# Sums of SBUF operands to VectorE, a changed product order and later memory values in a one-core decoder block

## The chip, the cores and the metric

The kernel runs on one core of a Trainium2 chip as one launch. The metric is device time in microseconds (us): 2584.59 us is the median of three runs (2582.75 to 2585.81). Engines are named as in the profile: PE (TensorE matmuls), PEld (its weight loads), DVE (VectorE), ACT (ScalarE), POOL (GpSimd), SP (the queue that issues DMAs).

## The reference, cut to what matters

One decoder block over 1024 tokens of width 1024, everything in fp32:

```python
x = x + 0.5 * swiglu(rmsnorm(x, ffn1_norm), ffn1_w_gate, ffn1_w_up, ffn1_w_down)      # FFN1, width 2816
x = x + hybrid_mixer(rmsnorm(x, mix_norm), ...)     # two attentions, gates, output projection
x = x + memory_cross_attention(rmsnorm(x, mem_q_norm), rmsnorm(mem, mem_kv_norm), ...)  # 256 memory tokens
x = x + 0.5 * swiglu(rmsnorm(x, ffn2_norm), ffn2_w_gate, ffn2_w_up, ffn2_w_down)      # FFN2
return rmsnorm(x, final_norm)
# swiglu: (silu(h @ w_gate) * (h @ w_up)) @ w_down;  memory: k, v = split(mem_n @ w_kv)
```

## The kernel before, in words

Every matrix product is made of three matmuls: each operand is split into a rounded part (an ACT copy, "hi") and the rest (a DVE subtraction, "lo"), and `mm3` (L375 to L377) multiplies hi by hi, hi by lo and lo by hi. Such a subtraction is called a split below.

The FFN projections use a scheme with seven products in place of eight (Strassen's, in Winograd's manner). Its left operand is the weights, its right operand the normalised tokens, each cut into 2 x 2 blocks. A block sum is needed for most products: of weights (`left_sums`, tile ws, then split into wf), of tokens (`norm_forms`, tile fs, then split into F, the "forms"), and in the down projection of weights again (tile da) and of gated results (tile gs). `sum_on` (L485 to L493) makes such a sum and lets the planner choose POOL or DVE. The token halves are tiles 0 to 3 and 4 to 7. Products 3 and 5 need forms of the second half alone (tiles R), product 4 and 2 the first half (tiles xs), products 1, 6 and 7 both.

`ffn_up` runs 11 steps; each step makes a gate projection (called g below) and an up projection (u) of one pair of column groups by `seven`, so 14 products of 12 matmuls of 512 columns: g3 g5 g4 g2 g1 g6 g7, then u3 to u7 in the same manner. After a product DVE or ACT takes its bank on (vt L535, L541, L545; sg L596, L599). `ffn_down` has seven stages of 11 such units for four banks. Before FFN1, `memory_kv` normalises the 256 memory tokens (xn, mT), makes eight key units (each 24 matmuls of 256 columns, results cc to DRAM) and two value groups (each 48 matmuls of 512 columns). Before FFN2, `out_proj` adds the cross attention to x tile by tile (x L1327), and each finished tile is normalised (ACT square, POOL rstd L439 and L440, DVE xn L444), transposed on PE (T), copied and turned into forms.

The order on each engine is no loop order. Every operation goes to a planner (`Plan`) with an assumed cost per engine and a rank, its due time, which advances with the assumed matmul times. `Plan.order` takes the operation with the lowest rank among those that could start next on the engine that comes free first, within 60 ns, and looks for free buffers in pools (`TAGS`, `POOLS`). Each engine then runs its list strictly in order, and so does the DMA queue SP. The lines that set it here are these:

```python
self.plan.op({"POOL": 2.9 * n + 50, "DVE": 1.04 * n + 157}, f, reads, writes, self.r if rank is None else rank)  # sum_on
for f in self.memory_kv(40.0): f()                 # keys and values, before the tokens
```

Of the kernel before, what the change touches and what calls it, by code (L numbers as in the profile page):

```python
# [10 lines left out]
F32 = mybir.dt.float32  # L11
# [8 lines left out]
P = 128  # L20
# [141 lines left out]
class Plan:  # L162
# [152 lines left out]
class Block:  # L315
# [46 lines left out]
    def dve(self, ns, run, reads, writes, rank=None):  # L362
        self.plan.op({"DVE": ns}, lambda _: run(), reads, writes, self.r if rank is None else rank)
# [39 lines left out]
    def weight(self, key, lead=14.0, pool=False):  # L403
# [20 lines left out]
    def rms(self, x, g, out, parts=1):  # L424

        nc, n = self.nc, D // parts
        st = self.buf("sm")
        cut = lambda b, j: b()[:, j * n:(j + 1) * n]
        key = lambda j: j if parts > 1 else None
        for j in range(parts):  # L430
            def square(j=j):

                nc.scalar.activation(cut(out, j), cut(x, j), AF.Square, scale=1.0 / math.sqrt(D), accum_out=st()[:, j:j + 1])
            self.act(n, square, [(x, key(j))], [(out, key(j)), (st, j)], sbuf=True, acc=True)

        def rstd():
            if parts > 1:
                nc.gpsimd.tensor_tensor(st()[:, 0:1], st()[:, 0:1], st()[:, 1:2], op=ALU.add)
            nc.gpsimd.tensor_scalar_add(st()[:, 2:3], st()[:, 0:1], EPS)  # L439
            nc.gpsimd.tensor_tensor(st()[:, 3:4], st()[:, 2:3], self.mhalf, op=ALU.pow)  # L440
        self.pool(425 + 220 * parts, rstd, [], [st])
        for j in range(parts):
            def scale(j=j):
                nc.vector.scalar_tensor_tensor(cut(out, j), cut(x, j), st()[:, 3:4], cut(g, j), op0=ALU.mult, op1=ALU.mult)  # L444
            self.dve(1.042 * n + 130, scale, [x, st, g], [(out, key(j))])

    def norm_T(self, x, g, put, writes, key):

        xn = self.buf("xn")
        self.rms(x, g, xn)  # L450
# [35 lines left out]
    def sum_on(self, n, out, a, b, sign, reads, writes, rank=None):  # L486

        nc = self.nc
        op = ALU.add if sign > 0 else ALU.subtract

        def f(en):
            (nc.vector if en == "DVE" else nc.gpsimd).tensor_tensor(out(), a(), b(), op=op)  # L492
        self.plan.op({"POOL": 2.9 * n + 50, "DVE": 1.04 * n + 157}, f, reads, writes, self.r if rank is None else rank)  # L493

    def left_sums(self, key0, key1, lead=12.0):
# [4 lines left out]
        for b, key in zip(raw, (key0, key1)):  # L500
            self.dma(524288, lambda b=b, key=key: nc.sync.dma_start(b(), self.io["w"][self.index[key]]), [], [b], self.r - lead - 8)
        quarter = lambda ij: raw[ij[0]]()[:, ij[1] * 512:ij[1] * 512 + 512]

        def make(i):
# [9 lines left out]
            self.dve(690, lambda: nc.vector.tensor_sub(w()[:, 512:1024], val(), w()[:, 0:512].bitcast(F32)),  # L514
# [4 lines left out]
    def seven(self, key0, key1, F, use):  # L519
# [3 lines left out]
        make = self.left_sums(key0, key1)  # L523
# [21 lines left out]
        self.dve(690, lambda: nc.vector.tensor_add(v(), x(), v()), [x], [(vt, 0)])  # L545
        product(6, y, False)
        self.dve(690, lambda: sub(d, y), [y, (vt, 0)], [(vt, 1)])
        use(1, 1, d, [(vt, 1)])
        product(7, z, False)
        self.dve(690, lambda: sub(v, z), [z], [(vt, 0)])  # L550
        use(0, 0, v, [(vt, 0)])

    def norm_forms(self, x, g, F, t):
# [3 lines left out]
        self.rms(x, g, xn)  # L557
# [13 lines left out]
        for i in (5, 3) if half else (4, 2, 1, 6, 7):  # L571
            parts = F.SUMS[i]
            src = [(F.raw[4 * ij[1] + t % 4], ij[0]) for ij in parts[:2]]
            if len(parts) == 1:
                val, rd = lambda parts=parts: part(parts[0]), src
            else:
                s = self.buf("fs")
                self.sum_on(512, s, lambda parts=parts: part(parts[0]), lambda parts=parts: part(parts[1]), parts[2], src, [s])
                val, rd = s, [s]
# [3 lines left out]
                       [(b, t % 4) for b in F.t[i][1]], count=2, sbuf=True)  # L583


    def ffn_up(self, n, F):
# [4 lines left out]
        for c in range(H):  # L591
# [6 lines left out]
            def up(i, j, view, reads, sg=sg, at=at):  # L598
                self.dve(690, lambda: nc.vector.tensor_mul(at(i, j), at(i, j), view()), reads, [(sg[i], j)])  # L599
            self.seven(("g" + n, c), ("g" + n, c + H), F, gate)  # L600
            self.seven(("u" + n, c), ("u" + n, c + H), F, up)
            for i, parts in self.LEFT.items():
# [9 lines left out]
                self.dma(262144, lambda i=i, c=c, val=val: nc.sync.dma_start(gd[i]()[c], val()), rd, [(gd[i], c)])  # L612
        return gd

    def ffn_down(self, n, gd, x, done):
# [10 lines left out]
        def load(i, k, m, lead=10.0):  # L626
# [18 lines left out]
            for b, tag in ((raw, "gf"), (src[0], "df")):  # L645
# [3 lines left out]
                self.dve(1.04 * w + 157, lambda b=b, hl=hl: nc.vector.tensor_sub(  # L649
# [26 lines left out]
        def into(t, bank, tb, ch, s):  # L676
            def f():
                xs = x[tb]()[:, ch * 512:ch * 512 + 512]
                stt(xs, bank[t](), xs, s)
            self.dve(690, f, [bank[t]], [(x[tb], ch)])  # L680
# [6 lines left out]
        stage(3, z, True, lambda t: self.dve(690, lambda: stt(v(t), z[t](), v(t), 0.5), [z[t]], [vk(t)]))  # L687
        stage(4, y2, True, lambda t: self.dve(690, lambda: stt(v(t), y2[t](), v(t), 0.5), [y2[t]], [vk(t)]))
# [11 lines left out]
    def memory_kv(self, lead):  # L700
# [4 lines left out]
        g = self.gain("mem_kv_norm")  # L705
        for t in range(2):
# [16 lines left out]
        def values(ch):  # L723
            pv = [self.buf("mm") for _ in range(2)]
# [693 lines left out]
    def run(self):  # L1418
# [23 lines left out]
        for f in self.memory_kv(40.0):  # L1442
            f()
        r = self.r
        self.r = 2.0
        g = self.gain("ffn1_norm", 0.0)
        x = load(lambda t: io["x"][t], order=late, lead=2.0, step=2.0)
# [8 lines left out]
        gd = self.ffn_up("1", F)  # L1456
# [27 lines left out]
        self.out_proj("mo", o, x, done, late=True)  # L1484
# [20 lines left out]
G0 = 3  # L1505
# [22 lines left out]
```

## Time and profile before

| | us |
|---|---|
| median of three runs | 2584.59 |
| the profiled execution | 2588.4 |
| its span, first to last instruction | 2586.4 |
| PE busy | 2522.5 (98%) |
| DVE busy | 1664.6 (64%) |
| ACT busy | 1180.9 (46%) |
| POOL busy | 619.3 (24%) |

All times in rows are from the span's start. A timeline row gives start, duration, engine, line, operation, out<-in, count, and in brackets the idle time before it with what ended it. Durations of instructions that follow each other overlap by up to 0.08 us, so the time that one takes on its engine is the distance to the next start. PEclk is the granted clock of TensorE: 1.00 is the upper of its two levels, 2.4 GHz, and 0.5 the lower, 1.2 GHz.

### The profile page before, as it was taken

The page shows a single profiled execution, that of the slowest core. Times are in us where ns is not written, and L with a number is a line of the kernel's source. Part 1 is how long each engine was busy: PE and PEld are TensorE (multiplying, and loading weights), DVE is VectorE, ACT ScalarE, POOL GpSimd, SP SyncE. Part 2 cuts the span into 40 slices and gives each one's busy share as a digit, 9 for nine tenths or more (in the row PEclk, how much of TensorE's full clock was granted, in tenths as well). Part 3 has the DMA queues.
Part 4 walks back from the last instruction along what each step waited for, and adds up shares of the span by engine and source line. Part 5 has one row for each costly group of instructions (what it writes and reads, how often), then busy time and mean ns, then how long its engine had stood idle before and what let it go on. Part 6 is the DMA issues. An engine that isn't in the chain of part 4 may idle for free.

```text
span 2586.4 us, 34955 instructions
## 1 busy us (share of the span) xinstructions
PE 2522.5 (98%) x12613; PEld 2132.7 (82%) x12613; DVE 1664.6 (64%) x3120; ACT 1180.9 (46%) x2352; POOL 619.3 (24%) x590
## 2 busy tenths in 40 slices
PE   7899999999999999999999999999998999999998
PEld 6688888888788888898888888888876888888887
DVE  8755556667765477788766766344576556557566
ACT  6422232334445567777776753233443232233433
POOL 5643344331200001111000003000034334332313
PEclk9999999999999999999999999999998999999999
DMA  7233233696722110210212344241112223327964
GB/s 280 98 114 114 78 131 118 205 369 225 266 82 83 45 58 30 72 63 19 79 53 82 116 137 155 82 147 57 50 74 86 97 103 106 123 93 271 343 234 164
DMA packets 137485, 329.90 MB, mean 128 GB/s; under 512 B 14656, under 2 KB 18096, under 8 KB 137184
## 3 DMA queue, kind: packets, MB, share of 16 engines
q1 hardware_dynamic: 137248, 327.47, 36.5%
q8 instruction: 99, 1.62, 0.3%
q14 instruction: 74, 0.61, 0.1%
q0 software_dynamic: 64, 0.20, 0.0%
HBM read 254.17 MB, written 75.02 MB: 127 GB/s over the span
## 4 chain that ended last, share of the span: by engine, by line
PE 89%; DVE 3%; ACT 2%; DMA 1%; issue 1%; POOL 0%; SPq 0%; DVEq 0%; POOLq 0%; ACTq 0%
PE z L375 11%; PE z L376 11%; PE z L377 11%; PE mm L375 7%; PE mm L376 7%; PE mm L377 7%; PE y L376 5%; PE y L375 5%; PE y L377 5%; PE T L381 4%; PE pv L1124 4%; PE acc L377 2%; PE acc L375 2%; PE acc L376 2%; PE s L1049 2%; PE s L1050 2%
## 5 line engine op out<-in xcount | busy, mean ns | idle before, releaser
L375 PE MATMUL z<-F,wf 128*128 128x512 f32 x1232 | 483.1, 392 | 15.0 <-ACT wf L513 5.0
L377 PE MATMUL z<-F,wf 128*128 128x512 f32 x1232 | 482.0, 391 | 3.5 <-DVE wf L514 3.5
L376 PE MATMUL z<-F,wf 128*128 128x512 f32 x1232 | 482.6, 392 | 2.5 <-DVE F L397 2.4
L492 POOL TENSOR_TENSOR ws<-wa 128x512 f32<-128x512 f32 x197 | 285.7, 1465 | 507.6 <-DVE wf L514 333.6
L375 PEld LDWEIGHTS z<-F,wf 128*128 128x128 f32 x1232 | 232.8, 189 | 66.7 <-ACT wf L513 5.5
L375 PE MATMUL mm<-h,w 128*128 128x512 f32 x704 | 286.8, 407 | 0.0
L377 PE MATMUL mm<-h,w 128*128 128x512 f32 x704 | 276.5, 393 | 0.0
L376 PE MATMUL mm<-h,w 128*128 128x512 f32 x704 | 276.4, 393 | 0.0
L377 PEld LDWEIGHTS z<-F,wf 128*128 128x128 f32 x1232 | 232.7, 189 | 52.7 <-DVE wf L514 4.6
L376 PEld LDWEIGHTS z<-F,wf 128*128 128x128 f32 x1232 | 232.8, 189 | 52.2 <-DVE F L397 4.0
L376 PE MATMUL y<-df,gf 128*128 128x512 f32 x616 | 239.9, 389 | 1.1 <-DVE df L649 1.1
L375 PE MATMUL y<-df,gf 128*128 128x512 f32 x616 | 240.4, 390 | 0.0
L377 PE MATMUL y<-df,gf 128*128 128x512 f32 x616 | 239.9, 389 | 0.0
L514 DVE TENSOR_TENSOR wf<-ws,wf 128x512 fp32r<-128x512 f32 x220 | 170.7, 777 | 48.8 <-ACT wf L513 48.8
L397 DVE TENSOR_TENSOR pt<-T,pt 128x512 fp32r<-128x512 f32 (+1 forms) x264 | 156.2, 614 | 68.4 <-ACT pt L390 67.3
L390 ACT CAST pt<-T 128x512 fp32r<-128x512 f32 (+1 forms) x264 | 132.3, 528 | 77.5 <-PE T L381 75.5
L1077 ACT ACTIVATE p<-p,sm 128x128 f32<-128x128 f32 (+7 forms) x192 | 143.4, 747 | 46.3 <-DVE sm L1147 43.8
L377 PEld LDWEIGHTS mm<-h,w 128*128 128x128 f32 x704 | 132.6, 188 | 29.7
L513 ACT CAST wf<-ws 128x512 fp32r<-128x512 f32 x220 | 131.8, 619 | 47.4 <-PE z L377 45.5
L376 PEld LDWEIGHTS mm<-h,w 128*128 128x128 f32 x704 | 133.6, 190 | 18.8
L375 PEld LDWEIGHTS mm<-h,w 128*128 128x128 f32 x704 | 133.3, 189 | 19.0
L413 DVE TENSOR_TENSOR w<-wr,w 128x1024 fp32r<-128x1024 f32 x95 | 121.4, 1289 | 40.4 <-ACT w L409 38.7
(254 smaller groups left out, 5042.3 us busy)
## 6 DMA issues: line engine op xcount, KB each, us to landing
da<-in_w_dram SPq DMA_DIRECT2D x264, 256.0 KB, 5.9
wr<-in_w_dram SPq DMA_DIRECT2D x95, 512.0 KB, 4.7
wa<-in_w_dram SPq DMA_DIRECT2D x88, 512.0 KB, 3.9
dg<-gd SPq DMA_DIRECT2D x70, 512.0 KB, 6.0
gd<-gs SPq DMA_DIRECT2D x110, 256.0 KB, 2.1
xd<-x SPq DMA_DIRECT2D x24, 512.0 KB, 2.6
x<-xd SPq DMA_DIRECT2D x24, 512.0 KB, 5.9
gd<-sg SPq DMA_DIRECT2D x44, 256.0 KB, 2.1
```

What stands on the lines that cost most here:

```text
L375: mm(out, a[0], b[0], start=first, stop=False, skip_group_check=more)
L376: mm(out, a[0], b[1], start=False, stop=False, skip_group_check=more)
L377: mm(out, a[1], b[0], start=False, stop=last, skip_group_check=more)
L381: self.nc.tensor.transpose(out, src, self.ident[0:k, 0:k])
L390: nc.scalar.copy(h, s)
L397: nc.vector.tensor_sub(l, s, h.bitcast(F32))
L413: self.dve(1135, lambda: nc.vector.tensor_sub(lo(), raw(), hi().bitcast(F32)), [raw, hi], [lo], rank=r + 4)
L492: (nc.vector if en == "DVE" else nc.gpsimd).tensor_tensor(out(), a(), b(), op=op)
L513: self.act(512, lambda: nc.scalar.copy(w()[:, 0:512], val()), rd, [(w, 0)], sbuf=True, rank=rank + 3)
L514: self.dve(690, lambda: nc.vector.tensor_sub(w()[:, 512:1024], val(), w()[:, 0:512].bitcast(F32)), rd + [(w, 0)], [(w, 1)], rank=rank + 3)
L1077: nc.scalar.activation(p[e]()[:, 0:row[e]], p[e]()[:, 0:row[e]], AF.Exp, bias=m[e]()[:, j:j + 1], scale=-1.0, accum_out=l()[:, e:e + 1])
L1124: mm(pv()[:, 0:256], v, y()[:, b * 256:b * 256 + 256], start=unit["fresh"], stop=stop and y is lo)
```

## The change

It has four parts. All sums of two SBUF operands go to DVE, with the assumed costs of DVE operations made smaller. In `ffn_up` the first step makes g3, g5, u3 and u5 before the rest (`apart`, `AHEAD`), and reads the first weight unit a second time for that. The forms of the first half have later due times (`LATER`), and `rms` tells the planner that the normalised tile is 1 us later (`slack`, in `norm_T` and `norm_forms`). The memory's normalised tokens are written to DRAM (md); the keys are made first, and each value group reads the tokens back and runs inside FFN1, ahead of steps 2 and 3.

```diff
-    "F": ("u", 28), "R": ("u", 4), "wa": ("u", 4), "wf": ("u", 6), "sg": ("u", 4), "vt": ("u", 2),
-    "da": ("u", 6), "dg": ("u", 3), "df": ("u", 6), "gf": ("u", 6), "vb": ("u", 2), "xs": ("u", 3),
+    "F": ("u", 28), "R": ("u", 4), "wa": ("u", 4), "wf": ("u", 6), "sg": ("u", 4), "vt": ("u", 4),
+    "da": ("u", 6), "dg": ("u", 3), "df": ("u", 6), "gf": ("u", 6), "vb": ("u", 2), "xs": ("u", 4),
...
     def norm_T(self, x, g, put, writes, key):
-        self.rms(x, g, xn)
+        self.rms(x, g, xn, slack=1000.0)
...
-        def f(en):
-            (nc.vector if en == "DVE" else nc.gpsimd).tensor_tensor(out(), a(), b(), op=op)
-        self.plan.op({"POOL": 2.9 * n + 50, "DVE": 1.04 * n + 157}, f, reads, writes, self.r if rank is None else rank)
+        self.dve(1.04 * n + 70, lambda: nc.vector.tensor_tensor(out(), a(), b(), op=op), reads, writes, rank)
...
-    def seven(self, key0, key1, F, use):
-        make = self.left_sums(key0, key1)
+    def seven(self, key0, key1, F, use, apart=False):
+        make = self.left_sums(key0, None if apart else key1)
...
         product(5, z, False)
         use(0, 1, z, [z])
+        yield
+        if apart:
+            make = self.left_sums(key0, key1)
         product(4, y, True)
-        self.dve(690, lambda: nc.vector.tensor_add(v(), y(), v()), [y], [(vt, 0)])
+        self.dve(603, lambda: nc.vector.tensor_add(v(), y(), v()), [y], [(vt, 0)])
...
     def norm_forms(self, x, g, F, t):
-            parts = F.SUMS[i]
+            parts, rank = F.SUMS[i], self.r + LATER.get(i, 0.0)
...
     def ffn_up(self, n, F, between={}):
+        rows = [parts(c) for c in range(H)]
+        early = {c: [next(rows[c]) for _ in range(2)] for c in range(AHEAD)}
+        for c in range(AHEAD):
+            for s in early[c]:
+                next(s)
+        for c in range(H):
+            between.get(c, lambda: None)()
+            for j in range(2):
+                s = early[c][j] if c < AHEAD else next(rows[c])
+                for _ in s:
+                    pass
+            next(rows[c])
...
     def memory_kv(self, lead):
+        for s, j in ((s, j) for j in range(2) for s in range(2)):
+            self.dma(524288, lambda s=s, j=j: nc.sync.dma_start(md[s][j](), mT[s][j]().bitcast(F32)), [mT[s][j]], [md[s][j]])
...
         def values(ch):
+            mT = [[self.buf("mT", F32R) for _ in range(2)] for _ in range(2)]
+            for s, j in ((s, j) for j in range(2) for s in range(2)):
+                self.dma(524288, lambda s=s, j=j: nc.sync.dma_start(mT[s][j]().bitcast(F32), md[s][j]()), [md[s][j]], [mT[s][j]],
+                         self.r - 12)
...
-        for f in self.memory_kv(40.0):
+        keys = self.memory_kv(0.0)
+        values = [keys.pop(), keys.pop()][::-1]
+        for f in keys:
             f()
...
-        gd = self.ffn_up("1", F)
+        gd = self.ffn_up("1", F, {2: values[0], 3: values[1]})
...
+G0, AHEAD = 3, 1
+LATER = {4: 8.0, 2: 11.0, 1: 14.0, 6: 17.0, 7: 20.0}
```

How this moves instructions is seen best on DVE. The first place is the start of FFN1, where the last form splits stand. Before, the queue has the splits of forms (F), mixed with weight splits (wf); the first results of a product (vt) come only after the last F:

```order
L397 TENSOR_TENSOR F<-fs,F 128x2x128 x8
L514 TENSOR_TENSOR wf<-wa,wf 128x512
L397 TENSOR_TENSOR cc<-mm,cc 128x512
L397 TENSOR_TENSOR F<-xs,F 128x2x128 x2
L397 TENSOR_TENSOR F<-fs,F 128x2x128 x2
L514 TENSOR_TENSOR wf<-ws,wf 128x512
L492 TENSOR_TENSOR fs<-xs,R 128x512
L397 TENSOR_TENSOR F<-fs,F 128x2x128 x2
L514 TENSOR_TENSOR wf<-wa,wf 128x512
L397 TENSOR_TENSOR F<-fs,F 128x2x128 x4
```

Now, in the same place, sums of weights (ws) and of tokens (fs) stand in the queue too, and the results of u5 (sg) and g4 (vt) stand ahead of the last forms:

```order
L488 TENSOR_TENSOR ws<-wa 128x512
L397 TENSOR_TENSOR F<-fs,F 128x2x128 x2
L511 TENSOR_TENSOR wf<-ws,wf 128x512
L488 TENSOR_TENSOR fs<-xs,R 128x512 x3
L397 TENSOR_TENSOR F<-xs,F 128x2x128 x2
L602 TENSOR_TENSOR sg<-sg,z 128x512
L397 TENSOR_TENSOR F<-fs,F 128x2x128 x2
L511 TENSOR_TENSOR wf<-ws,wf 128x512
L488 TENSOR_TENSOR fs<-xs,R 128x512
L542 TENSOR_TENSOR vt<-z,vt 128x512
```

So products run on PE between the forms instead of behind them. The second place is the start of FFN2, where the last token tile is added (x<-acc,x), normalised (xn) and copied (xs). Before, 24 form splits and three sums stand between xn of the tile before and that add:

```order
L444 SCALAR_TENSOR_TENSOR xn<-x,sm,gain 128x1024
L397 TENSOR_TENSOR F<-fs,F 128x2x128 x8
L492 TENSOR_TENSOR fs<-xs,R 128x512
L397 TENSOR_TENSOR F<-fs,F 128x2x128 x2
L397 TENSOR_TENSOR F<-xs,F 128x2x128 x2
L397 TENSOR_TENSOR F<-fs,F 128x2x128 x4
L492 TENSOR_TENSOR fs<-xs 128x512
L492 TENSOR_TENSOR fs<-xs,R 128x512
L397 TENSOR_TENSOR F<-fs,F 128x2x128 x8
L1327 TENSOR_TENSOR x<-acc,x 128x512
L514 TENSOR_TENSOR wf<-ws,wf 128x512
```

Now three split pairs, a sum and a copy stand between them:

```order
L441 SCALAR_TENSOR_TENSOR xn<-x,sm,gain 128x1024
L397 TENSOR_TENSOR F<-fs,F 128x2x128 x2
L488 TENSOR_TENSOR fs<-xs 128x512
L397 TENSOR_TENSOR F<-fs,F 128x2x128 x2
L569 COPY xs<-T_18593 128x512
L397 TENSOR_TENSOR F<-fs,F 128x2x128 x2
L1353 TENSOR_TENSOR x<-acc,x 128x512
L397 TENSOR_TENSOR F<-fs,F 128x2x128 x2
L488 TENSOR_TENSOR fs<-xs,R 128x512
L488 TENSOR_TENSOR fs<-xs 128x512
L511 TENSOR_TENSOR wf<-ws,wf 128x512
L441 SCALAR_TENSOR_TENSOR xn<-x,sm,gain 128x1024
```

The add of the last tile has moved ahead of most forms of the tiles before it.

## Rows read from the trace of the kernel before

**Rows 1.** The page's first part: busy time, share and instructions by engine.
```profile
PE 2522.5 (98%) x12613; PEld 2132.7 (82%) x12613; DVE 1664.6 (64%) x3120; ACT 1180.9 (46%) x2352; POOL 619.3 (24%) x590
```
**Rows 2.** Busy time by stretch: length, PE, PEld, DVE, ACT, POOL, PEclk, DMA, GB/s.
```profile
0.00:65.00 65.00, 46.58 (x313) 43.58 (x313) 52.43 (x73) 44.60 (x90) 32.97 (x34) 0.99 0.76 278
65.00:130.00 65.00, 52.62 (x215) 41.33 (x214) 50.04 (x68) 30.43 (x66) 39.31 (x24) 0.93 0.29 98
...
195.00:260.00 65.00, 65.00 (x288) 53.84 (x287) 37.96 (x54) 15.71 (x30) 24.97 (x17) 1.00 0.33 114
...
520.00:585.00 65.00, 65.00 (x289) 53.83 (x288) 42.46 (x36) 27.10 (x31) 18.99 (x8) 1.00 1.01 373
```
**Rows 3.** Waits of PE over the span: us in total, times, longest.
```profile
PE T L381 <- DVE xn L444: 26.0, 7, 8.1
```
**Rows 4.** Timeline of DVE from the start into FFN1.
```profile
6.77 1.28 DVE L444 SCALAR_TENSOR_TENSOR xn<-m,sm,gain 128x1024 f32<-128x1024 f32 x1 [5.61 <-POOL sm L440]
...
11.56 1.22 DVE L413 TENSOR_TENSOR w<-wr,w 128x1024 fp32r<-128x1024 f32 x1
...
49.11 0.75 DVE L397 TENSOR_TENSOR F<-R,F 128x256 fp32r<-128x256 f32 x2
49.78 2.94 DVE L397 TENSOR_TENSOR F<-fs,F 128x256 fp32r<-128x256 f32 x2
...
54.45 1.28 DVE L492 TENSOR_TENSOR fs<-xs,R 128x512 f32<-128x512 f32 x2
...
82.49 6.02 DVE L397 TENSOR_TENSOR F<-fs,F 128x256 fp32r<-128x256 f32 x8
...
95.83 2.47 DVE L397 TENSOR_TENSOR F<-fs,F 128x256 fp32r<-128x256 f32 x2 [1.62 <-ACT F L390]
...
133.25 0.68 DVE L535 TENSOR_TENSOR vt<-vt,z 128x512 f32<-128x512 f32 x1
```
**Rows 5.** Timeline of POOL beside the eight splits at 82.49.
```profile
82.11 1.60 POOL L492 TENSOR_TENSOR fs<-xs,R 128x512 f32<-128x512 f32 x1 [1.43 <-DVE F L397]
...
86.85 1.38 POOL L492 TENSOR_TENSOR fs<-xs,R 128x512 f32<-128x512 f32 x1 [1.03 <-DVE F L397]
```
**Rows 6.** Timeline of PE in the keys.
```profile
40.03 0.28 PE L377 MATMUL mm<-mT,w 128*128 128x256 f32 x1
40.15 0.28 PE L375 MATMUL mm<-mT,w 128*128 128x256 f32 x1
```
**Rows 7.** Timeline of DVE at the start of FFN2.
```profile
1921.10 0.68 DVE L1327 TENSOR_TENSOR x<-acc,x 128x512 f32<-128x512 f32 x1
...
1941.22 0.68 DVE L1327 TENSOR_TENSOR x<-acc,x 128x512 f32<-128x512 f32 x1
...
1944.59 1.28 DVE L444 SCALAR_TENSOR_TENSOR xn<-x,sm,gain 128x1024 f32<-128x1024 f32 x1
...
1954.11 4.92 DVE L397 TENSOR_TENSOR F<-fs,F 128x256 fp32r<-128x256 f32 x8
...
1988.90 0.68 DVE L535 TENSOR_TENSOR vt<-vt,z 128x512 f32<-128x512 f32 x1
```
**Rows 8.** Busy time by stretch at the start of FFN2.
```profile
1930.00:1940.00 10.00, 5.30 (x16) 3.60 (x14) 10.00 (x19) 5.05 (x17) 4.50 (x4) 0.83 0.00 2
1940.00:1950.00 10.00, 5.71 (x20) 4.42 (x20) 4.72 (x9) 4.57 (x8) 3.20 (x3) 0.66 0.14 54
1950.00:1960.00 10.00, 5.16 (x11) 3.45 (x12) 9.63 (x14) 4.72 (x13) 6.50 (x5) 0.74 0.29 104
```
**Rows 9.** Groups by line over the span: busy, mean ns, idle before.
```profile
L492 POOL TENSOR_TENSOR ws<-wa 128x512 f32<-128x512 f32 x197 | 285.7, 1465 | 507.6 <-DVE wf L514 333.6 <-DMA wa<-in_w_dram 118.6 <-PE mm L376 21.2
L492 POOL TENSOR_TENSOR da<-da 128x1024 f32<-128x1024 f32 (+1 forms) x31 | 78.6, 2536 | 240.9 <-DMA da<-in_w_dram 124.9 <-DVE df L649 54.1 <-ACT gf L647 44.8
L397 DVE TENSOR_TENSOR F<-fs,F 128x256 fp32r<-128x256 f32 x80 | 46.6, 639 | 1.8 <-ACT F L390 1.8
L492 DVE TENSOR_TENSOR da<-da 128x1024 f32<-128x1024 f32 (+1 forms) x29 | 34.1, 1176 | 37.1 <-DMA da<-in_w_dram 37.0
```

More of the change, by code (lines that the diff above doesn't have):

```diff
@@ L360, in act, with dve @@
                      hold=hold)
-    def dve(self, ns, run, reads, writes, rank=None):
-        self.plan.op({"DVE": ns}, lambda _: run(), reads, writes, self.r if rank is None else rank)
+    def dve(self, ns, run, reads, writes, rank=None, delay=0.0):
+        self.plan.op({"DVE": ns}, lambda _: run(), reads, writes, self.r if rank is None else rank, delay)
     def pool(self, ns, run, reads, writes, rank=None):
@@ L401, in split, with weight @@
         self.dve(1.04 * n + 70 * count, g, list(reads) + list(wh), wl, rank=rank)
-    def weight(self, key, lead=14.0, pool=False):
+    def weight(self, key, lead=14.0):
         nc = self.nc
@@ L421, in gain, with rms @@
         return g
-    def rms(self, x, g, out, parts=1):
+    def rms(self, x, g, out, parts=1, slack=0.0):
         nc, n = self.nc, D // parts
@@ L444, in scale @@
                 nc.vector.scalar_tensor_tensor(cut(out, j), cut(x, j), st()[:, 3:4], cut(g, j), op0=ALU.mult, op1=ALU.mult)
-            self.dve(1.042 * n + 130, scale, [x, st, g], [(out, key(j))])
+            self.dve(1.042 * n + 130, scale, [x, st, g], [(out, key(j))], delay=slack)
     def norm_T(self, x, g, put, writes, key):
         xn = self.buf("xn")
-        self.rms(x, g, xn)
+        self.rms(x, g, xn, slack=1000.0)
         for j in range(2):
@@ L500, in left_sums @@
         for b, key in zip(raw, (key0, key1)):
+            if key is None:
+                continue
             self.dma(524288, lambda b=b, key=key: nc.sync.dma_start(b(), self.io["w"][self.index[key]]), [], [b], self.r - lead - 8)
@@ L556, in norm_forms @@
         xn = self.buf("xn")
-        self.rms(x, g, xn)
+        self.rms(x, g, xn, slack=1000.0)
         raw = F.raw[t] = self.buf("R" if half else "xs")
@@ L679, in f @@
                 stt(xs, bank[t](), xs, s)
[L680 removed]
+            self.dve(603, f, [bank[t]], [(x[tb], ch)])
         def plus_v(t, tb, ch):
@@ L704, in memory_kv @@
         mT = [[self.buf("mT", F32R) for _ in range(2)] for _ in range(2)]
-        g = self.gain("mem_kv_norm")
+        g = self.gain("mem_kv_norm", lead + 0.5)
         for t in range(2):
@@ L710, in memory_kv @@
             self.norm_T(m, g, put, lambda s, j: [mT[s][j]], t)
+        md = [[self.dram([P, 1024], f"md{s}{j}") for j in range(2)] for s in range(2)]
+        for s, j in ((s, j) for j in range(2) for s in range(2)):
+            self.dma(524288, lambda s=s, j=j: nc.sync.dma_start(md[s][j](), mT[s][j]().bitcast(F32)), [mT[s][j]], [md[s][j]])
         at = lambda k, a, b: [mT[s][k // 4]()[:, (k % 4) * 256 + a:(k % 4) * 256 + b] for s in range(2)]
@@ L1310, in combine_b, with out_proj @@
         return y
-    def out_proj(self, name, y, x, done, late=False):
+    def out_proj(self, name, y, x, done, halves=(range(NT),)):
         nc = self.nc
-        for ch in range(2):
+        for ts, ch in ((ts, ch) for ts in halves for ch in range(2)):
             ws = [self.weight((name, ch, j), 16.0 - 4 * j) for j in range(4)]
-            for t in [4, 5, 6, 7, 0, 1, 2, 3] if late else range(NT):
+            for t in ts:
                 po, hf, off = self.buf("acc"), t // 4, (t % 4) * P
@@ L1440, in then @@
             return H, done
-        for f in self.memory_kv(40.0):
-            f()
[L1444 to L1447, printed above, removed]
+        self.r = -20.0
+        keys = self.memory_kv(0.0)
+        values = [keys.pop(), keys.pop()][::-1]
+        self.r = 0.0
+        for f in keys:
+            f()
+        r, self.r = self.r, -13.0
+        g = self.gain("ffn1_norm", 0.5)
+        x = load(lambda t: io["x"][t], order=late, lead=0.0, step=1.5)
         F = Forms(self, "F")
         for j, t in enumerate(late):
-            self.r = 6.0 + 4.0 * j
+            self.r = 3.0 * j - 2.0
             self.norm_forms(x[t], g, F, t)
@@ L1483, in run @@
         F, done = then(x, "ffn2_norm", True, Forms(self, "F"), self.norm_forms)
-        self.out_proj("mo", o, x, done, late=True)
+        self.out_proj("mo", o, x, done, (late,))
         gd = self.ffn_up("2", F)
```

36 lines of the change are left out of this document (17 added, 19 removed).

## The prediction, made before the result

> **What bounds the kernel now.** I read the page's first part, then the busy time by stretch, then the waits of PE, then the timelines of the two places where PE is not full. PE is busy 2522.5 of 2586.4 us [rows 1], so almost all of the span is matmul time, which the change does not shorten: every product of before is still there. In the steady part of FFN1 one stretch of 65 us holds 288 matmuls without a gap at a granted clock of 1.00 [rows 2], so a matmul of 512 columns takes 65/288 = 0.226 us, a product of 12 takes 2.71 us, and a step of 14 products 37.9 us. No edit can gain there. What can be gained is in the two places where forms are made. In the first two stretches PE is busy 46.58 and 52.62 of 65 us, 30.8 us idle, while DVE is busy 52.43 and 50.04 us [rows 2]; the largest wait of PE, 26.0 us, is for normalised tiles from DVE [rows 3]. At the start of FFN2 the three stretches from 1930 to 1960 hold 16, 20 and 11 matmuls, with the granted clock at 0.83, 0.66 and 0.74 [rows 8]: 47 x 0.226 = 10.6 us of work at the upper clock in 30 us, so about 19.4 us are lost, more than the 13.8 us that PE is idle, because it also works at the lower of its two levels. In both places the end is set by the DVE queue: the last form is split, and only then do the last products of the first step follow.
>
> **Prices.** From [rows 4], by the distance to the next start: a pair of splits of 256 columns 0.67 us (49.11 to 49.78), a 512-column operation 0.60 us (54.45, two in 1.20), a normalisation 1.20 us (1.28 less 0.08), a weight split of 1024 columns 1.14 us. A 256-column key split I take as half a pair, 0.33 us. These are prices without POOL beside them. With it they are longer: the eight splits at 82.49 took 6.02 us where four pairs cost 2.7, beside three sums on POOL (82.11 to 88.2, first and last shown) [rows 4, 5].
>
> **Start of FFN1.** Counted in the new DVE queue, from the first normalisation to the last form split: 10 normalisations (12.0), 8 weight splits of the keys (9.1), 32 pairs of splits (28 of forms, 4 of memory; 21.4), 8 key splits (2.6), and 47 operations of 512 columns (20 token sums, 9 weight sums, 12 weight splits, 3 copies, 2 vt, 1 sg; 28.2): 73.3 us. The first normalisation starts at 6.77 [rows 4], since the first loads are the same in kind; I add 4 us of waits for loads and for ACT, an estimate. The last form is then ready at 84, against 98.3 before [rows 4]. The new queue has more sums than the old one, but it is rid of the eight weight splits of the values (9.1) and of the stretching. By then PE has done the keys (192 matmuls of 256 columns, 0.12 us apart [rows 6], 23.0 us), the products g3, u3, g5, u5, g4, g2, and, since the list interleaves them, u4 and g1. Left are g6, three quarters of u1, g7, u2, u6, u7 and rests, of which g6 and u1 reach a little past 84; g7 ends at 88, and the last 40 matmuls or so take 9 us more, so step 0 ends at 97. Before it ended just ahead of the last vt at 133.25 [rows 4], with the values already made. They now follow in steps 2 and 3 as 96 matmuls, 21.7 us. So 97 + 21.7 = 118.7 against 133.2, -14.5. I take -12, because the 4 us of waits is the least certain number. Ends: -17 without waits, 0 if the chain is as late as before.
>
> **Start of FFN2.** The add of the third tile of the first half is at 1921.10 and PE reaches the last tile 6 us later; but its add is done at 1941.22, behind 24 splits, so it is normalised at 1944.59 and its last eight splits end at 1959.0 [rows 7]. In the new queue the add stands behind three pairs, a sum and a copy. From 1921.10 to the last form split it holds 2 normalisations (2.4), 19 pairs (12.7) and 31 operations of 512 columns (18.8), 33.9 us, plus 2 us of waits: 1957, only 2 us earlier. The gain is not there but in what PE can do meanwhile: g3, u3, g5 and u5 need only the second half, and g4, g2, u4, g1 and g6 follow as their forms come, since the forms are now made in the order of need. g6 ends at about 1958.3, then come g7, u2, u1, u6, u7: 5 x 2.71 = 13.6, end of step 0 at 1971.9. Before it was 1988.8 [rows 7], so -16.9. PE still waits in two or three places of 1.5 to 3 us, where the lower clock may return as in [rows 8]; I charge one product more, 2.7 us, and take -14. Ends: -19.4 (all that is lost), -2 (only the last form's time).
>
> **What costs nothing.** In steady FFN work DVE has per step 41 operations of 512 columns (14 wf, 10 ws, 8 vt, 4 sg, 5 gs), 24.7 of 37.9 us, so the 197 weight sums that leave POOL [rows 9] lie beside PE's work. In the down projections a pair of units gives PE 5.4 us and DVE at most three operations of 1024 columns, 3.4 us. The cover is gone if one of them waits at the head of the queue, see the fourth case. The values in steps 2 and 3 need four weight splits each (4.6 us of DVE, in a stretch with 37.96 of 65 us busy [rows 2]) and 4 MB of tokens read back in all, in a stretch at 114 GB/s against 373 GB/s in another [rows 2]: nothing; at worst one wait per value group like the 4.3 us idle in 1940 to 1950 [rows 8], +9. On SP the four writes of the tokens stand ahead of two token tiles of the first half, which are needed late. The slack of the normalisations: nothing.
>
> **Sum.** -12 - 14 = -26. The profiled execution took 2588.4 us (span 2586.4 and 2.0 around it), which gives 2562; it is 3.8 above the median of 2584.59, and against the median the forecast is 2559.
>
> **The other ways.**
> Second case: the start gains nothing. The queue has keys, second-half tiles and weight sums in one strict order, and each may wait for a load or for PE's first keys; DVE was busy 52.43 of the first 65 us [rows 2], which speaks against it. Then only FFN2 gains: 2584.6 - 14 = 2571.
> Third case: the splits stay long. If their stretching does not come from POOL, the 80 form splits, all of them in these two starts, cost 639 ns and not half of 0.75 us [rows 4, 9], 80 x 0.264 = 21 us more on the two chains: 2559 + 21 = 2580. The Trainium skill's page "Perfetto Trace Analysis", section "Optimizing Scalar/DVE Operations", speaks for moving work to GpSimd where DVE is saturated, which DVE is here, and against this change; it adds that the two share an SBUF read port, so that moving may not help. By the first half the time would be near this case's; the row at 82.49 agrees with the second half.
> Fourth case, slower: sums of down weights at the head of the DVE queue. The 31 that POOL made waited 124.9 us for their loads, 4.0 each; the 29 on DVE waited 37.0, 1.3 each [rows 9]. If the moved ones wait as long as on POOL, each holds DVE 4.0 + 1.1 us, where a pair of units leaves about 1.9 (DVE is busy 42.46 of 65 us there, with loads at 373 GB/s [rows 2], so 35% of 5.4 is free): 3.2 us late. From 8 of the 31 on the gain is used up; with half of them +48: 2559 + 48 = 2607. Against it: DVE comes to them later than an idle POOL, as the 1.3 us show.
> Fifth case: no change. The values collide with the steps they are put in (+9), and the queues lose the rest; 2584.
>
> **How the numbers follow.** Forecast 0.70 (its own range 2549 to 2568), second case 0.12, third 0.06, fourth 0.07, fifth 0.05. About 0.2%, 5 us, is what can be told from no change: below 2579.4 is faster. The third case lies on that line and is shared out. Faster 0.85, the same 0.08, slower 0.07. The low end is both places at their ends (2584.6 - 17 - 19 = 2549); the high end takes in the second case and part of the third, 2577.
>
> **What would show it.** Right: the last vt of step 0 near 97 in FFN1 and near 1963 in FFN2 (1988.9 less 26), form splits at 0.37 us each with POOL nearly silent, no idle time of PE in steps 2 and 3 beyond a microsecond, and PE full in both down projections. Wrong: form splits still above 0.5 us; DVE waiting for loads of da for more than 80 us; PE waiting for value weights or for mT; or DVE idle by more than 10 us ahead of the last form of FFN1.

## The result, and the profile after

The changed kernel takes 2556.9 us (median of 4 runs, 2555.2 to 2558.8) where the kernel before takes 2584.5 (2582.8 to 2585.8): a ratio of 0.9894 with a 95% interval of 0.9877 to 0.9911, 27.7 us less. The prediction said 2559. Its profiled execution has a span of 2557.0 us, against 2586.4.

The first part of the page after, to be read against [rows 1]: VectorE has taken over POOL's work (+68 us for 468 us less), and PE's 12613 matmuls take 8 us less, with fewer of them at the lower clock level.

```profile
PE 2514.6 (98%) x12613; PEld 2127.8 (83%) x12613; DVE 1732.6 (68%) x3412; ACT 1183.2 (46%) x2350; POOL 151.0 (6%) x300
```

Busy time by stretch after, columns as in [rows 2], and at the start of FFN2 as in [rows 8]:

```profile
0.00:65.00 65.00, 46.72 (x312) 42.78 (x313) 52.42 (x92) 49.34 (x106) 21.03 (x27) 0.98 0.81 302
65.00:130.00 65.00, 61.45 (x255) 50.12 (x254) 54.99 (x101) 24.15 (x52) 0.00 (x0) 0.94 0.33 110
195.00:260.00 65.00, 65.00 (x289) 53.83 (x288) 41.37 (x67) 19.45 (x37) 0.00 (x0) 1.00 0.41 141
520.00:585.00 65.00, 65.00 (x289) 53.81 (x288) 42.45 (x43) 29.08 (x34) 0.19 (x2) 1.00 1.02 375
...
1920.00:1930.00 10.00, 7.73 (x36) 5.73 (x34) 9.68 (x21) 8.30 (x19) 0.29 (x1) 1.00 0.17 55
1930.00:1940.00 10.00, 8.50 (x36) 6.70 (x37) 10.00 (x22) 4.04 (x11) 0.00 (x0) 1.00 0.00 0
1940.00:1950.00 10.00, 10.00 (x46) 8.29 (x45) 9.60 (x18) 5.18 (x11) 0.00 (x0) 1.00 0.51 176
1950.00:1960.00 10.00, 10.00 (x46) 8.29 (x45) 8.73 (x15) 1.98 (x4) 0.00 (x0) 1.00 0.17 61
```

In the second stretch PE does 61.45 us in place of 52.62, and from 1930 to 1960 128 matmuls in place of 47, at a granted clock of 1.00. The same work lies 13 us earlier in the new kernel; over the 30 us that lie as far behind the third tile's add (1916.9 to 1946.9) it is 120 matmuls. The full stretches are as full as before: the sums now on VectorE lie beside PE's work there.

Waits of PE, us in total, times, longest, to [rows 3]. Before, those for a bank that a vt has to free:

```profile
PE z L375 <- ACT vt L537: 4.3, 2, 3.7
PE z L375 <- DVE vt L541: 2.0, 1, 2.0
```

And after:

```profile
PE T L381 <- DVE xn L441: 15.6, 5, 10.0
PE z L375 <- DVE vt L542: 4.8, 2, 3.6
PE z L375 <- ACT vt L535: 4.7, 2, 3.0
```

The wait for normalised tiles went from 26.0 to 15.6 us, and 10.0 of it is the first one, for the first tile of all. The waits for a bank of z that a vt has to free went from 6.3 to 9.5 us.

Groups by line after, to [rows 9]: a form split costs 422 ns where it cost 639, and the sums of down weights wait 35.5 us for loads (37.0 with the ten of 512 columns), as long as the 29 on DVE did before.

```profile
L397 DVE TENSOR_TENSOR F<-fs,F 128x256 fp32r<-128x256 f32 x80 | 29.6, 422 | 0.0
L488 DVE TENSOR_TENSOR da<-da 128x1024 f32<-128x1024 f32 x50 | 61.1, 1222 | 41.7 <-DMA da<-in_w_dram 35.5 <-issue 6.2
```

The timeline of DVE after, at the two starts, to [rows 4, 7]:

```profile
8.68 1.28 DVE L441 SCALAR_TENSOR_TENSOR xn<-m,sm,gain 128x1024 f32<-128x1024 f32 x1 [7.52 <-POOL sm L437]
...
86.42 2.77 DVE L397 TENSOR_TENSOR F<-fs,F 128x256 fp32r<-128x256 f32 x8
...
101.68 0.69 DVE L533 TENSOR_TENSOR vt<-vt,z 128x512 f32<-128x512 f32 x1
...
1916.71 0.68 DVE L1353 TENSOR_TENSOR x<-acc,x 128x512 f32<-128x512 f32 x1
...
1920.32 1.28 DVE L441 SCALAR_TENSOR_TENSOR xn<-x,sm,gain 128x1024 f32<-128x1024 f32 x1 [0.46 <-POOL sm L437]
...
1942.79 0.77 DVE L397 TENSOR_TENSOR F<-fs,F 128x256 fp32r<-128x256 f32 x2
...
1960.03 0.69 DVE L533 TENSOR_TENSOR vt<-vt,z 128x512 f32<-128x512 f32 x1
```

Eight splits in a row take 2.77 us at 86.42; the eight at 82.49 took 6.02 before. The last tile's add is at 1916.71, not 1941.22, and step 0 of FFN2 ends at 1960, not 1989; 13.1 us of each of the last two differences were gained before the third tile's add, as the next rows show.

Where the 29.4 us of the two profiled executions went is read off three instructions: the last gated result of FFN1 (sg), the add of tile 2 ahead of FFN2 (x<-acc; 1921.10 in [rows 7]) and the last add of the last stage (x<-y). Before, the first and the third:

```profile
517.13 0.68 DVE L599 TENSOR_TENSOR sg<-sg,vt 128x512 f32<-128x512 f32 x1
...
2578.82 0.69 DVE L674 SCALAR_TENSOR_TENSOR x<-y,x 128x512 f32<-128x512 f32 x1
```

And all three after:

```profile
507.75 0.69 DVE L602 TENSOR_TENSOR sg<-sg,vt 128x512 f32<-128x512 f32 x1
...
1907.98 0.69 DVE L1353 TENSOR_TENSOR x<-acc,x 128x512 f32<-128x512 f32 x1 [0.89 <-PE acc L377]
...
2549.42 0.69 DVE L690 SCALAR_TENSOR_TENSOR x<-y,x 128x512 f32<-128x512 f32 x1
```

The gain is 9.4 us to the end of FFN1's steps, 13.1 - 9.4 = 3.7 in the middle, and 29.4 - 13.1 = 16.3 from there. The runs below are cut in the same way:

| kernel | median, us | FFN1 | middle | FFN2 |
|---|---|---|---|---|
| the change | 2556.9 | -9.4 | -3.7 | -16.3 |
| sums alone on VectorE | 2563.3 | -12.0 | -3.9 | -9.2 |
| change, sums POOL or VectorE | 2596.4 | +10.3 | -2.4 | +0.3 |
| change, POOL reads beside the forms | 2588.3 | +5.8 | -4.5 | -3.6 |
| change, POOL reads in steps 2 to 10 | 2556.1 | -11.7 | -7.1 | -16.2 |
| change, no early products | 2562.5 | -10.1 | -6.5 | -10.6 |
| change, forms not in order of need | 2571.9 | -4.4 | -4.2 | -8.0 |
| change, no slack | 2561.8 | -5.9 | -3.6 | -17.3 |
| change, values first | 2552.6 | -13.6 | -5.1 | -16.0 |
| values first, gain as before | 2553.9 | -14.1 | -4.9 | -16.3 |
| change, values ahead of steps 0 and 2 | 2557.4 | -10.9 | -3.4 | -16.2 |
| values first, two steps early | 2547.3 | -14.2 | -5.8 | -21.2 |

The columns come from one execution each, and all are taken against an execution of the kernel before that took 3.8 us more than its median (after: 1.9 more), so they need not add up to the difference of the medians. Parts that an edit does not touch still differ by up to 3.4 us (the middle, with and without POOL's reads in the steps), so only larger differences are read from them.

### The profile page after: what moved, and what is told of

Same layout as the page of the kernel before. It is cut to its first block, busy times and chain, and to the rows that moved or that the text cites. A ratio compares the mean times of both kernels' runs of the same rounds, so it can differ in the third digit from the quotient of the medians.

```text
span 2557.0 us, 34726 instructions
## 1 busy us (share of the span) xinstructions
PE 2514.6 (98%) x12613; PEld 2127.8 (83%) x12613; DVE 1732.6 (68%) x3412; ACT 1183.2 (46%) x2350; POOL 151.0 (6%) x300
## 4 chain that ended last, share of the span: by engine, by line
PE 91%; DVE 4%; ACT 2%; DMA 1%; issue 1%; POOL 0%; SPq 0%; DVEq 0%; POOLq 0%; ACTq 0%
PE z L375 10%; PE z L376 10%; PE z L377 10%; PE mm L375 8%; PE mm L376 8%; PE mm L377 8%; PE y L376 5%; PE y L377 5%; PE y L375 5%; PE T L381 5%; PE pv L1149 4%; PE acc L377 2%; PE acc L375 2%; PE acc L376 2%; PE s L1074 2%; PE s L1075 2%
## 5 line engine op out<-in xcount | busy, mean ns | idle before, releaser
L375 PE MATMUL z<-F,wf 128*128 128x512 f32 x1232 | 482.5, 392 | 10.1 <-DVE vt L542 4.8
L397 DVE TENSOR_TENSOR pt<-T,pt 128x512 fp32r<-128x512 f32 (+1 forms) x264 | 156.1, 614 | 68.8 <-ACT pt L390 67.8
L511 DVE TENSOR_TENSOR wf<-ws,wf 128x512 fp32r<-128x512 f32 x220 | 150.7, 686 | 39.7 <-ACT wf L510 39.4
L488 DVE TENSOR_TENSOR ws<-wa 128x512 f32<-128x512 f32 x220 | 149.6, 687 | 7.0 <-DMA gd<-gs 3.2
L1149 PE MATMUL pv<-pt,V 128*128 128x256 f32 x848 | 142.1, 292 | 2.3 <-DVE pt L397 1.4
```

Source lines behind the costliest of these rows:

```text
L375: mm(out, a[0], b[0], start=first, stop=False, skip_group_check=more)
L397: nc.vector.tensor_sub(l, s, h.bitcast(F32))
L488: self.dve(1.04 * n + 70, lambda: nc.vector.tensor_tensor(out(), a(), b(), op=op), reads, writes, rank)
L511: self.dve(603, lambda: nc.vector.tensor_sub(w()[:, 512:1024], val(), w()[:, 0:512].bitcast(F32)), rd + [(w, 0)], [(w, 1)], rank=rank + 3)
L1149: mm(pv()[:, 0:256], v, y()[:, b * 256:b * 256 + 256], start=unit["fresh"], stop=stop and y is lo)
```

## The experiments

Two theories stood at first. A: the order of products and forms brings the gain. B: most of it comes from a POOL that no longer reads beside VectorE. The kernel before was timed beside each set of runs (2585.1, 2585.2, 2585.4).

**Sums on either engine, all else as changed.**

```diff
-        self.dve(1.04 * n + 70, lambda: nc.vector.tensor_tensor(...), reads, writes, rank)
+        self.plan.op({"POOL": 2.9 * n + 50, "DVE": 1.04 * n + 157}, f, reads, writes, ...)
```

> The changed kernel with one part undone: the planner may again give a sum to POOL or DVE. Theory A (both starts end when the VectorE chain ends; POOL's sums stretch the splits beside them): form splits go back from 422 ns to about 600, but some 50 operations of 0.6 us leave the two chains; net 5 to 7 us longer at each start, 2567 to 2571 us, the reordering keeps the rest. Theory B (the whole gain is the silence of POOL, the new order adds little): back to about 2580. If POOL's stretching did not matter: 2557 or less.

Measured 2596.4 (2594.0 to 2599.0), ratio 1.0044 (1.0031 to 1.0056): slower than the kernel before, and beyond both theories. The form splits, in the groups by line of this run, are longer than before:

```profile
L397 DVE TENSOR_TENSOR F<-fs,F 128x256 fp32r<-128x256 f32 x80 | 54.1, 727 | 0.0
```

So the parts of the new order, with POOL at work in them, gain nothing. The planner makes each list anew when POOL may take sums, so this run does not part POOL's reads from the order that comes with them; the run with POOL's reads beside the forms does.

**The sums alone, in the kernel before.**

```diff
-        self.plan.op({"POOL": 2.9 * n + 50, "DVE": 1.04 * n + 157}, f, reads, writes, ...)
+        self.dve(1.04 * n + 70, lambda: nc.vector.tensor_tensor(...), reads, writes, rank)
```

> The kernel before with one part done: every sum on DVE at the new assumed cost, old order and old place of the values. Theory A: form splits at about 420 ns, but products still wait for the last form; the starts gain 5 us each, 2573 to 2577 us. Theory B: nearly the whole gain, 2558 to 2562. If sums at the head of the DVE queue wait for loads in the down projections: above 2585.

Measured 2563.3 (2562.8 to 2568.2), ratio 0.992 (0.9906 to 0.9933): 21.8 of the 27.7 us, with splits of 419 ns. That is B's side, a little above its range. In FFN1 this one edit gains at least as much as the whole change. What is left for the other parts is FFN2. No run takes back the bigger pools (vt from 2 to 4 buffers, xs from 3 to 4) or the smaller assumed cost of the vt operations by themselves, so their share of it is not known.

**POOL reads beside the forms.** The sharpest test: VectorE keeps every sum, and the order of PE, VectorE, ACT and SP is the same, instruction for instruction. Only POOL has more to do, and nobody waits for it.

```diff
+                    for a in (0, 256):      # behind each token sum fs
+                        nc.gpsimd.tensor_tensor(self.spare, part(parts[0])[:, a:a + 256],
+                                                part(parts[1])[:, a:a + 256], op=ALU.add)
...
```

> The changed kernel; behind each of its 40 token sums POOL adds the same two operands once more, in two halves of 256 columns, into a tile that nobody reads. All other engines keep their order and their work. Theory A (the gain of the sums on VectorE comes from a silent POOL, because POOL's reads stretch DVE's operations with two SBUF inputs): the F<-fs splits go from 422 ns to 550 to 650 ns, 80 x 0.13 to 0.23 = 10 to 18 us longer, so 2566 to 2576, with both first steps late by about half of that each. Theory B (POOL's sums only came late, their reads disturb little): splits stay at 420 to 450 ns and the time at 2555 to 2560.

Measured 2588.3 (2585.1 to 2592.2), ratio 1.0009 (1.0 to 1.0018): 78 us more of POOL's time, on which nobody waits, take the whole gain. That is about as much work as POOL had before: at the start of FFN1 it is busy 60.1 of the first 130 us here, 72.3 in the kernel before [rows 2]. Groups by line of this run, then the timelines of POOL and of DVE at the start of FFN2:

```profile
L398 DVE TENSOR_TENSOR F<-fs,F 128x256 fp32r<-128x256 f32 x80 | 42.6, 580 | 0.0
```
```profile
1919.49 4.36 POOL L584 TENSOR_TENSOR spare<-xs,R 128x256 f32<-128x256 f32 x4
...
1946.67 9.41 POOL L584 TENSOR_TENSOR spare<-xs,R 128x256 f32<-128x256 f32 x10
```
```profile
1921.21 1.21 DVE L582 TENSOR_TENSOR fs<-xs,R 128x512 f32<-128x512 f32 x1
1922.35 0.68 DVE L1359 TENSOR_TENSOR x<-acc,x 128x512 f32<-128x512 f32 x1
1922.95 0.68 DVE L570 COPY xs<-T 128x512 f32<-128x512 f32 x1
...
1947.67 1.22 DVE L582 TENSOR_TENSOR fs<-xs,R 128x512 f32<-128x512 f32 x1
1948.82 1.81 DVE L398 TENSOR_TENSOR F<-fs,F 128x256 fp32r<-128x256 f32 x2
1950.56 1.21 DVE L582 TENSOR_TENSOR fs<-xs 128x512 f32<-128x512 f32 x1
1951.69 1.81 DVE L398 TENSOR_TENSOR F<-fs,F 128x256 fp32r<-128x256 f32 x2
1953.42 1.21 DVE L512 TENSOR_TENSOR wf<-ws,wf 128x512 fp32r<-128x512 f32 x1
1954.55 1.81 DVE L398 TENSOR_TENSOR F<-fs,F 128x256 fp32r<-128x256 f32 x2
1956.29 0.67 DVE L608 TENSOR_TENSOR sg<-sg,z 128x512 f32<-128x512 f32 x1
1956.88 0.68 DVE L582 TENSOR_TENSOR fs<-xs,R 128x512 f32<-128x512 f32 x1
1957.48 0.75 DVE L398 TENSOR_TENSOR F<-xs,F 128x256 fp32r<-128x256 f32 x2
```

While POOL's ten additions run (1946.67 to 1956.08), a sum or a split of 512 columns on VectorE takes 1.21 us and a pair of form splits 1.81; as soon as POOL is done they take 0.68 and 0.75. The add and the copy at 1922.35 and 1922.95, beside the four additions before, take 0.68: they read PSUM and at most one operand in SBUF. Nothing waits for these additions. The normalisations' own small POOL operations, which stand between them, held VectorE up by 0.46 to 0.77 us at the start of FFN2, 0.46 in the change; and at the start of FFN1 VectorE's timeline shows no idle time from 23 to 98 us, so only longer operations can make its queue late there. So it is POOL's work beside VectorE that costs.

By the distance of starts, from 1947.67 to 1956.29, a sum takes 1.14 us instead of 0.60 and a split 0.87 instead of 0.34: long or short, each operation is held up by about 0.53 us. Nine operations that need 3.8 us alone (three of 0.60, six of half of 0.67) take 8.6, beside nine additions. POOL's 0.94 us for one addition contain waits of its own: two additions of the next run, in a stretch where VectorE has nothing with two SBUF inputs to do, take 1.56 us together, which is 0.74 for one and 0.82 from start to start.

```profile
210.47 1.56 POOL L513 TENSOR_TENSOR spare<-wa 128x256 f32<-128x256 f32 x2
```

So one operation and one addition take turns. The Trainium skill's page "SBUF — State Buffer", section "SBUF: two separate sides", says that a VectorE operation with two SBUF inputs and a GpSimd one that reads SBUF shut each other out; the trace agrees on which operations are hit. It says further that the loser waits for the whole instruction of the other; the trace shows 0.53 us of the 0.74 that the addition lasts when it is undisturbed.

The time lost, 31.5 us, is more than the expected 10 to 18, and more than the splits' own 13 us: the sums and normalisations are stretched as well, so that VectorE is busy 36.8 us longer in all (1769.4 for 1732.6), and PE, left waiting, falls to its lower level. Two rows by stretch of this run, to those after at 1940 and 1950:

```profile
1940.00:1950.00 10.00, 4.50 (x12) 3.25 (x12) 10.00 (x14) 4.95 (x13) 7.46 (x9) 0.83 0.10 41
1950.00:1960.00 10.00, 5.25 (x12) 3.76 (x12) 9.50 (x14) 2.10 (x6) 5.61 (x7) 0.54 0.00 0
```

**POOL reads in the steady steps.** The same second addition, behind the weight sums of steps 2 to 10 (360 instructions).

```diff
+                    for h in (0, 256) if key0[1] >= 2 else ():      # behind each weight sum ws
+                        nc.gpsimd.tensor_tensor(self.spare, quarter(parts[0])[:, h:h + 256], ...)
```

> The changed kernel; behind each weight sum of FFN steps 2 to 10 POOL adds the same two operands once more, in two halves of 256 columns, into a tile that nobody reads; all other queues stay as they are. Theory A (POOL stretches DVE's operations, and that costs time only where DVE sets the end): weight splits and sums go from 686 to 800 ns or more, some 20 operations a step by 0.3 us = 6 us, DVE up to 31 of 37.9 us, the time unchanged, 2554 to 2560. Rival (in steady FFN work the stretched splits come too late for PE, a product every 2.7 us): over 2563.

Measured 2556.1 (2553.1 to 2558.5): unchanged. The sums went from 687 to 888 ns, the splits from 686 to 752 only, less than expected. In this stretch, to the third row by stretch after, VectorE is 10.3 us busier and PE as full:

```profile
195.00:260.00 65.00, 65.00 (x289) 53.80 (x288) 51.67 (x66) 20.94 (x39) 49.37 (x51) 1.00 0.38 133
```

So POOL's reads cost nothing in the steps where PE sets the pace, though VectorE is busy 72.1 us longer, and all of the gain at the two starts.

**The parts of the order.** Early products off (`AHEAD`), then the forms' later due times off (`LATER`), then the slack off:

```diff
-G0, AHEAD = 3, 1
+G0, AHEAD = 3, 0
```

> The changed kernel without the early products: step 0 makes g3 g5 g4 g2 g1 g6 g7 and then u3 to u7. Theory A (PE needs other products while forms are made): at both starts u3 and u5, 5.4 us of PE work, no longer lie in the gap; up to 5.4 us late at each, 2563 to 2568. Rival (the forms' chain alone sets the end of step 0, the other work of the list fills the gap anyway): 2555 to 2559.

Measured 2562.5 (2558.8 to 2563.8), +5.6. The loss is in FFN2 alone (-10.6 for -16.3: 5.7 us, the two products), while FFN1 has other work to fill the gap. A held for one of two places.

```diff
-LATER = {4: 8.0, 2: 11.0, 1: 14.0, 6: 17.0, 7: 20.0}
+LATER = {}
```

> The changed kernel with one due time for all forms of a tile of the first half. Theory A (the forms must come in the order of need): g4 and g2 wait for splits of forms 1, 6 and 7 of the tiles before, 3 products late at each start by 2 to 4 us: 2561 to 2566; DVE's add of the last tile before FFN2 goes later than 1916.7. Rival (the last form sets the end and it is ready at the same time): 2555 to 2559.

Measured 2571.9 (2568.8 to 2572.2), +15, where 4 to 9 were expected: 5 us in FFN1 and 8.3 in FFN2. DVE's add of the last tile is at 1925.14 and its normalisation nine microseconds behind it, where the change has 3.6:

```profile
1925.14 0.68 DVE L1353 TENSOR_TENSOR x<-acc,x 128x512 f32<-128x512 f32 x1
...
1934.39 1.28 DVE L441 SCALAR_TENSOR_TENSOR xn<-x,sm,gain 128x1024 f32<-128x1024 f32 x1
```

Of the parts taken out here it is the strongest, and without it the change is worse than the sums alone.

```diff
-        self.rms(x, g, xn, slack=1000.0)
+        self.rms(x, g, xn, slack=0.0)
```

> The changed kernel without the extra 1 us that the planner is told for a normalised tile. Theory A (it moves a few instructions and no time, as charged): 2555 to 2559. Rival (it gives the gain in the middle of the program, 2 us in the region of the mix norm and 2 us around the two output projections): 2559 to 2562.

Measured 2561.8 (2561.2 to 2563.5), +4.9. Both theories missed the place: the time is the rival's, but the middle is unchanged (-3.6), and 3.5 us are lost in FFN1, hardly more than the columns can tell. So the slack is worth some 5 us, and where it earns them is not settled.

**The place of the values.** Values at the start as before, without writing the tokens to DRAM and back:

```diff
...
-        gd = self.ffn_up("1", F, {2: values[0], 3: values[1]})
+        gd = self.ffn_up("1", F)      # values run in the loop over keys, from mT in SBUF
```

> The changed kernel with the values made at the start, before FFN1, as before (no write and read back of the memory tokens). Theory A as the prediction put it counts the values' weight splits as a load on the chain that was taken off: chain 11.5 us longer, but PE had 18 us idle in the first 65 us of the changed kernel and 21.7 us of value work could lie there, so the same sum read fully says 5 to 10 us faster, 2547 to 2552 us. Theory C (moving the values out of the start is what gave FFN1 its gain): slower by about 10, 2565 to 2570.

Measured 2552.6 (2551.1 to 2553.9), ratio 0.9874 (0.986 to 0.9887), 4.3 us faster than the change, nearly all of it in FFN1 (-13.6 for -9.4; the two other runs with values first show -14.1 and -14.2). From 60 to 80 us PE does 76 matmuls in this run and 42 in the change. So the values fill time in which PE is idle or slow in the change, and moving them out cost that.

Then the first value group ahead of step 0, the second ahead of step 2:

```diff
-        gd = self.ffn_up("1", F, {2: values[0], 3: values[1]})
+        gd = self.ffn_up("1", F, {0: values[0], 2: values[1]})
```

> The changed kernel with the first value group ahead of the rest of step 0 and the second ahead of step 2 (before: ahead of 2 and 3). PE idles and runs at the lower clock between 60 and 80 us, where products wait for forms. Theory A: 10.9 us of value matmuls fill that gap and cost DVE 4.6 us of weight splits; about 5 us faster, 2552 us. Theory C: the splits lengthen the chain by 4.6 us and the values are not early enough to fill anything, 2560 to 2562.

Measured 2557.4 (2555.6 to 2557.8), as the change. This program's output is wrong, for a reason that is not known, so it can't be used and is read only for where its work lies. The group does fill the gap, 64 matmuls at a granted clock of 1.00 from 60 to 75 us, but PE then waits 7.3 us from 76 to 90 for weight splits and a weight copy (4.8 for VectorE, 2.5 for ACT), where the change has no wait. That fits the rival's point that the added splits lengthen the chain; what was filled was lost again.

Values first, and the gain of the memory norm loaded behind the first memory tile, as in the kernel before:

```diff
...
-        g = self.gain("mem_kv_norm", lead + 0.5)
+        g = self.gain("mem_kv_norm", lead)
```

> Values at the start as in the run with values first (2552.6), and the gain of the memory norm loaded behind the first memory tile, as in the kernel before. Theory A (DVE's chain from the first normalisation sets the end of step 0): the first xn starts 1.9 us earlier, at 6.8, and the time falls by about as much, 2550 to 2551. Rival (loads set the pace later, so the start of the chain has slack): 2552 to 2554.

Measured 2553.9 (2551.4 to 2554.7), no gain. But the edit did not do what it was made for: the gain's load is still issued first, at 0.73, and the memory tile's at 1.18, where the kernel before issues the tile at 0.73. The first normalisation starts at 8.84 here and at 9.04 in the run with values first. It waits for that tile in all of them: ACT's square of it starts at 4.61 before and at 6.67 here, when the tile has landed. So the run does not decide between the two theories, and why the tile lands two microseconds later stays open.

**A faster version.** Values first, and the first two steps make their early products ahead:

```diff
...
-G0, AHEAD = 3, 1
+G0, AHEAD = 3, 2
```

> Values at the start, as in the run that had them first (2552.6), and the first two steps instead of one make g3, g5, u3 and u5 early. Theory A (PE's gaps that are left at the starts, 3.8 us from 1920 to 1940 and more in the first 130 us, take the four products more): 2547 to 2551. Rival (VectorE sets the pace there, and the weights of four products more stand in its queue ahead of forms): 2553 to 2558.

Measured 2547.3 (2546.9 to 2547.5), ratio 0.9853 (0.9838 to 0.9868), below the change's interval. Against values first (2552.6) the gain is in FFN2 (-21.2 for -16.0): its gap is closed. Two stretches of this run, to 7.73 and 8.50 of PE after:

```profile
1920.00:1930.00 10.00, 10.00 (x46) 8.29 (x45) 10.00 (x24) 7.88 (x20) 0.00 (x0) 1.00 0.00 1
1930.00:1940.00 10.00, 10.00 (x46) 8.24 (x45) 10.00 (x19) 3.96 (x9) 0.00 (x0) 1.00 0.28 105
```

## Why the prediction was right, point by point

**The bound** was read right: the full stretches stayed full, and most of the gain is in the two starts, 25.7 of the 29.4 us of the two profiled executions. That the total came within about 2 us is in part luck: FFN1 gave 2.6 us less than was taken, FFN2 2.3 more, and the middle 3.7 that were charged at nothing.

**Start of FFN1**, -12 (worked: -14.5), measured -9.4 to the end of the steps. Step 0 ended at 101.7, not 97; with the values' 21.7 us that is 123.4 for 118.7. DVE's chain was priced well: from the first normalisation to the end of the last split 80.4 us (8.68 to 89.1) for 77.3, though it began 1.9 us late. But this chain does not set the end any more. PE waits for nothing from 74.02 to the end of step 0; that step 0 ends 12.6 us behind the last split, close to the 13 worked, is chance. What made it late lies before: 3.0 and 3.6 us of waiting for banks, whose vt stand behind splits on ACT and DVE, and the clock behind each wait. The timeline of PE after:

```profile
63.22 0.80 PE L375 MATMUL z<-F,wf 128*128 128x512 f32 x1 [2.95 <-ACT vt L535]
...
74.02 0.80 PE L375 MATMUL z<-F,wf 128*128 128x512 f32 x1 [3.55 <-DVE vt L542]
74.62 0.63 PE L376 MATMUL z<-F,wf 128*128 128x512 f32 x1
75.04 0.63 PE L377 MATMUL z<-F,wf 128*128 128x512 f32 x1
...
80.14 0.39 PE L377 MATMUL z<-F,wf 128*128 128x512 f32 x1
```

Behind the second wait matmuls start 0.42 us apart, the lower level. From 74.02 to 80.14 there are 14, 6.12 us where 14 x 0.226 = 3.16 would do; with 7 from 63.22 to 66.37 the loss is 4.5 us, beside 6.5 of waiting. The prediction charged the clock in FFN2 (2.7 us), where it stayed at 1.00, and not here.

**Start of FFN2**, -14 (worked: -16.9), measured -16.3. From the add of tile 2 to the last form split the queue was counted at 35.9 us; it took 35.5 (1907.98 to 1943.5). To the end of step 0 the working has 50.8 us, measured 52.1 (to 1960.03); before it was 67.8. The worked value was the better one, since the charge for the clock fell away.

**The middle** was charged at nothing and gave 3.7 us. Every changed kernel shows 2.4 to 7.1 there, the one with sums on POOL too, so the runs do not say which part brings it. PE's wait for a normalised tile at the mix norm fell from 1.9 to 0.6 us; the rest stays open.

**What costs nothing.** Steady sums, down sums and value weights were hidden as said. From 130 to 280 us, where the values and steps 2 and 3 run, PE has no wait in the profile. But moving the values was not free: it cost 4.3 us, because at the start they lie partly in PE's idle time. The sum counted their 21.7 us in both orders as if they were work on the path, and their 9.1 us of weight splits as a gain for VectorE's chain. The slack, charged at nothing too, is worth some 5 us.

**The other ways.** The second case fell by the -9.4 in FFN1. The third needs splits that stay above 0.5 us; they cost 422 ns, and the run with POOL's reads shows why. Its price mixed two measures: 639 ns is the mean of single splits in the trace and 0.375 half of a merged pair; against the 422 ns measured it is 80 x 0.217 = 17 us, not 21. That run, with splits of 580 ns, lost 31.5, so the price left out what else is stretched. The Trainium skill's page "Perfetto Trace Analysis", section "Optimizing Scalar/DVE Operations", speaks for sharing work with GPSIMD where VectorE is saturated and warns that it might not help; in this kernel the warning holds, and more: sharing the sums cost 21.8 us. The fourth needed DVE to wait over 80 us for da; it waited 37.0. The fifth fell with the total.

The attribution in the sum was the weak point. The prediction treated the new order as the source of the FFN2 gain and the silent POOL as a price of 21 us if it failed. The runs show the reverse weights: sums alone give 21.8 us, the order and the early products give 7 more in FFN2, the values give 4 back, and the new order with POOL at work is 11.4 us slower than the old kernel. The parts don't add up to the whole; the runs fit the reading that the later ones gain only on top of the first.

## What to carry to other kernels

Ahead of moving work to an idle engine, ask what its reads do to its neighbour: look for the same instruction with two mean times in the trace, and see which engine runs in the longer case. Such a stretch cost nothing where TensorE sets the pace (72.1 us more on VectorE) and nearly its whole size in the short places where VectorE does (31.5 us for 36.8), so those places, not the mean, decide. Work that can run at any time belongs in the gap, and a move out of it is a cost, even where the new place has room.

## What was not expected of the hardware

Two things. An addition of 256 columns on POOL lasts 0.74 us when it is undisturbed and holds up VectorE by 0.2 us in the mean of steady steps ((1804.7 - 1732.6)/360, the busy time of DVE in the two kernels), but by 0.53 us, whatever the length of the operation, where VectorE has no gaps. And PE came back at the lower clock level behind waits of 2.95 and 3.55 us at the start of FFN1, while the granted clock stayed at 1.00 around waits of 1.8 and 1.3 us at the start of FFN2.
